# RMSNorm with gamma and Silu on one core: 64 KB runs in three buffers, gamma alone on VectorE, Silu by row with a scale, no look-ahead

## Chip, cores, metric

One core of a Trainium2 chip. The metric is the device time of one execution in microseconds (us).

## The reference, cut

```python
# x: 8 x 1024 x 2048 float32, gamma: 2048 float32, eps = 1e-5
rms = np.sqrt(np.mean(x ** 2, axis=-1, keepdims=True) + eps)
out = gamma * x / rms
return out * (1 / (1 + np.exp(-out)))          # Silu
```

There are 8192 rows of 8 KB. Every row is read once and written once: 67.1 MB in, 67.1 MB out. Nothing is reused except gamma.

## The kernel before

A block is 512 rows: four consecutive rows (32 KB) in each of 128 partitions, 4.2 MB. There are 16 blocks and six buffers. Loads are issued from ScalarE, stores from SyncE. The squares of a block are shared between ScalarE (`Square` with an accumulator) and VectorE; ScalarE takes the root, VectorE inverts it, VectorE multiplies by the reciprocal and gamma in one instruction per row, ScalarE applies Silu to two rows at a time.

```python
    J = 4
    BUFS = 6
    xb = x2.rearrange("(b p j) d -> b p (j d)", p=P, j=J)
    ...
    def load(b):
        xt = pool.tile([P, J * d], f32, name="xt")
        nc.scalar.dma_start(out=xt, in_=xb[b])
    ...
    def multiply(b):
        for j in range(J):
            nc.vector.scalar_tensor_tensor(out=row(b, j), in0=row(b, j), scalar=rstds[b][:, j:j + 1],
                                           in1=g, op0=ALU.mult, op1=ALU.mult)

    def silu(b):
        for h in range(0, J, 2):
            cols = slice(h * d, (h + 2) * d)
            nc.scalar.activation(out=blocks[b][:, cols], in_=blocks[b][:, cols], func=ACT.Silu)
        store(b)
    ...
        for b in range(last):                       # look-ahead: squares of b+1 before or beside block b
            loads = [b + 3] if BUFS <= b + 3 < nblk else []
            ...
            elif b < last - 1:
                squares_scalar(b + 1, loads)
                squares_vector(b + 1)
                root(b + 1)
                multiply(b)
                silu(b)
```

## Time and profile before

| | kernel before |
|---|---|
| time, median of 3 | 316.8 us (316.8 to 316.83) |
| span of the profile | 315.1 us |
| VectorE / ScalarE busy | 235.3 us (75%) / 213.8 us (68%) |
| DMA queues, share of 16 engines | 49.7% + 49.3% |

How to read it. A row of the 40 slices gives the busy share of an engine in each fortieth of the span, in tenths, 9 meaning 90% or more. The line of a DMA queue gives packets, MB, and the share of the 16 engines' time that its packets took. If the two queues together fill the span and the engines' rows have holes, the transfers set the time. The lines themselves stand in the prediction.

### The profile page before, as it was taken

How to read it: one execution, taken by the hardware profiler on the slowest of the kernel's cores; microseconds unless marked ns; L12 is line 12 of the kernel's file. 1: busy time of each engine (PE TensorE's matmuls, PEld its weight loads, DVE VectorE, ACT ScalarE, POOL GpSimd, SP SyncE). 2: the span in 40 equal slices, each digit the busy share in tenths (PEclk: the TensorE clock that was granted, in tenths of full speed). 3: DMA queues.
4: the chain of work that ended last, by engine and by line, in shares of the span. 5: the costliest groups of instructions: out<-in, count | busy, mean ns of one | idle time of the engine just before them, and what ended most of it. 6: DMA issues, size and time to landing. Idle time of an engine off the chain costs nothing.

```text
span 315.1 us, 436 instructions
## 1 busy us (share of the span) xinstructions
PE 2.1 (1%) x8; PEld 0.5 (0%) x8; DVE 235.3 (75%) x157; ACT 213.8 (68%) x136; POOL 0.2 (0%) x4
## 2 busy tenths in 40 slices
PE   0200000000000000000000000000000000000000
PEld 0000000000000000000000000000000000000000
DVE  0679597979995695957969489693995939999600
ACT  1349998972799258682687827877288768779910
POOL 0000000000000000000000000000000000000000
DMA  8999999999999999999999999999999999999996
GB/s 334 403 462 403 395 466 399 466 403 462 403 463 403 459 412 453 412 453 420 445 420 445 424 441 424 441 424 441 428 437 437 428 445 420 445 420 445 420 449 287
DMA packets 4618, 134.24 MB, mean 426 GB/s; under 512 B 516, under 2 KB 516, under 8 KB 520
## 3 DMA queue, kind: packets, MB, share of 16 engines
q10 hardware_dynamic: 2304, 67.11, 49.7%
q1 hardware_dynamic: 2312, 67.12, 49.3%
q14 instruction: 2, 0.02, 0.0%
HBM read 67.12 MB, written 67.11 MB: 426 GB/s over the span
## 4 chain that ended last, share of the span: by engine, by line
DMA 68%; DVE 14%; ACT 11%; issue 2%; ACTq 1%; DVEq 0%
DMA xt<-in_x_dram 68%; DVE xt L93 9%; DVE junk_v L74 5%; ACT xt L99 4%; ACT junk_a L66 3%; ACT xt L157 2%; ACT L83 1%; ACTq L190 1%; ACT L157 0%; ACT L99 0%; ACT rms L83 0%; DVE ss L74 0%; DVE rstd L88 0%; ACTq L55 0%; ACTq L83 0%
## 5 line engine op out<-in xcount | busy, mean ns | idle before, releaser
L93 DVE SCALAR_TENSOR_TENSOR xt<-xt,rstd,g 128x2048 f32<-128x2048 f32 x60 | 137.0, 2347 | 0.1
L99 ACT ACTIVATE xt<-xt 128x4096 f32<-128x4096 f32 x30 | 108.3, 3615 | 27.2 <-DVE xt L93 27.1
L74 DVE CUSTOM_DVE_ANT_0 junk_v<-xt 128x2048 f32<-128x2048 f32 x37 | 85.1, 2299 | 42.5 <-DMA xt<-in_x_dram 41.7
L66 ACT ACTIVATE junk_a<-xt 128x2048 f32<-128x2048 f32 x27 | 50.7, 1877 | 22.6 <-DMA xt<-in_x_dram 22.3
L83 ACT ACT_TABLE_LOAD x15 | 19.2, 1283 | 27.6 <-DVE ss L74 27.5
L99 ACT ACT_TABLE_LOAD x14 | 18.0, 1283 | 0.2
L118 DVE COPY g<-junk_v 128x2048 f32<-128x2048 f32 x1 | 2.3, 2292 | 9.4 <-PE junk_v L116 9.4
L88 DVE RECIPROCAL rstd<-rms 128x4 f32<-128x4 f32 x16 | 2.8, 174 | 8.3 <-ACT rms L83 8.3
L155 DVE TENSOR_TENSOR xt<-xt,g 128x2048 f32<-128x2048 f32 x4 | 8.9, 2279 | 0.0
L83 ACT ACTIVATE rms<-ss,eps_t 128x4 f32<-128x4 f32 x16 | 4.8, 297 | 5.7 <-DVE ss L74 5.5
L157 ACT ACTIVATE xt<-xt,rstd 128x2048 f32<-128x2048 f32 x4 | 7.7, 1990 | 0.0
L74 DVE DVE_READ_ACCUMULATOR2_ANT ss<- 128x1 f32 x37 | 5.2, 141 | 0.0
L66 ACT ACTIVATION_READ_ACCUMULATOR junk_a<-xt 128x1 f32 x27 | 5.0, 186 | 0.0
L111 ACT ACT_TABLE_LOAD x1 | 1.3, 1283 | 3.8 <-issue 3.8
L116 PE MATMUL junk_v<-grow,ones 1*128 1x512 f32 x8 | 2.1, 1130 | 8.2 <-DMA grow<-in_gamma_dram 8.2
L157 ACT ACT_TABLE_LOAD x1 | 1.3, 1283 | 0.0
L109 DVE MEMSET ones<- 128x128 f32 x1 | 0.2, 165 | 0.8 <-PEq L176 0.8
L116 PEld LDWEIGHTS junk_v<-grow,ones 1*128 1x128 f32 x8 | 0.5, 307 | 8.2 <-issue 8.2
L111 ACT ACTIVATE junk_a<-ones 128x1 f32<-128x1 f32 x1 | 0.2, 174 | 0.0
L176 POOL MEMSET const-bfloat16-1.0<- 128x1 bf16 x1 | 0.1, 101 | 0.0
L176 POOL MEMSET const-uint8-127<- 128x1 uint8 x1 | 0.1, 101 | 0.0
L176 POOL MEMSET const-float32-0.0<- 128x1 f32 x1 | 0.1, 98 | 0.2 <-issue 0.2
(2 smaller groups left out, 0.2 us busy)
## 6 DMA issues: line engine op xcount, KB each, us to landing
xt<-in_x_dram ACTq DMA_DIRECT2D x16, 4096.0 KB, 38.7
out_dram<-xt SPq DMA_DIRECT2D x16, 4096.0 KB, 29.0
grow<-in_gamma_dram SPq DMA_DIRECT2D x1, 8.0 KB
```

The source lines that it names most:

```text
L66: nc.scalar.activation(out=junk_a, in_=row(b, j), func=ACT.Square, accum_out=sss[b][:, j:j + 1])
L74: nc.vector.tensor_tensor_reduce(out=junk_v, in0=row(b, j), in1=row(b, j), scale=1.0, scalar=0.0, op0=ALU.mult, op1=ALU.add, accum_out=sss ...
L83: nc.scalar.activation(out=rms, in_=sss.pop(b), func=ACT.Sqrt, scale=1.0 / d, bias=eps_t)
L88: nc.vector.reciprocal(out=rstd, in_=rmss.pop(b))
L93: nc.vector.scalar_tensor_tensor(out=row(b, j), in0=row(b, j), scalar=rstds[b][:, j:j + 1], in1=g, op0=ALU.mult, op1=ALU.mult)
L99: nc.scalar.activation(out=blocks[b][:, cols], in_=blocks[b][:, cols], func=ACT.Silu)
L111: nc.scalar.activation(out=junk_a[:, 0:1], in_=ones[:, 0:1], func=ACT.Square)
L116: nc.tensor.matmul(junk_v[:, c * w:(c + 1) * w], ones[k:k + 1, :], grow[k:k + 1, :], start=True, stop=True)
L118: nc.vector.tensor_copy(out=g, in_=junk_v)
L155: nc.vector.tensor_mul(out=row(last, j), in0=row(last, j), in1=g)
L157: nc.scalar.activation(out=row(last, j), in_=row(last, j), func=ACT.Silu, scale=rstds[last][:, j:j + 1])
L190: with _tile.TileContext(nc) as tc:
```

## The change

It asks for longer runs in HBM (64 KB: eight rows per partition), fewer and larger transfers, fewer switches of ScalarE's tables, and a simpler order: load, squares, root, multiply, Silu, store, tile after tile, with no work on the next tile ahead of time. VectorE multiplies by gamma alone, two rows per instruction, and need not wait for the root; the reciprocal enters as the scale of Silu. The first and the last tile are cut in halves (and the last store in 4, 2, 2 rows).

```diff
-    J = 4
-    BUFS = 6
+    R = 8
+    BUFS = 3
+    xs = x2.rearrange("(s p r) d -> s p (r d)", p=P, r=R)
 ... (os likewise, for the output)
+    loads_of = [[R] for _ in range(nsup)]
+    stores_of = [[R] for _ in range(nsup)]
+    loads_of[0] = stores_of[0] = [4, 4]
+    loads_of[nsup - 1] = [4, 4]
+    stores_of[nsup - 1] = [4, 2, 2]
 ... (in load)
+        for lo, hi in pieces(loads_of[s]):
+            nc.scalar.dma_start(out=xt[:, cols(lo, hi)], in_=xs[s][:, cols(lo, hi)])
 ... (in group(s, lo, hi): squares of the first half of the rows on ScalarE, of the second on VectorE, root)
+        for r in range(lo, hi, 2):
+            if r == lo + 2:
+                nc.vector.reciprocal(out=rstd[:, 0:k], in_=rms[:, 0:k])
+            two = xt[:, cols(r, r + 2)].rearrange("p (r d) -> p r d", r=2)
+            nc.vector.tensor_mul(out=two, in0=two, in1=g.unsqueeze(1).to_broadcast([P, 2, d]))
+        for r in range(lo, hi):
+            row = xt[:, cols(r, r + 1)]
+            nc.scalar.activation(out=row, in_=row, func=ACT.Silu, scale=rstd[:, r - lo:r - lo + 1])
+            for a, b in pieces(stores_of[s]):
+                if b == r + 1:
+                    nc.sync.dma_start(out=os[s][:, cols(a, b)], in_=xt[:, cols(a, b)])
 ... (the loop)
+        for s in range(nsup):
+            for lo, hi in pieces(loads_of[s]):
+                group(s, lo, hi)
+            if s >= 1 and s + 2 < nsup:
+                load(s + 2)
```

More of the change, by code (lines that the diff above doesn't have):

```diff
@@ L31 @@
     n, d = x2.shape
-    J = 4
-    BUFS = 6
-    nblk = n // (P * J)
-    xb = x2.rearrange("(b p j) d -> b p (j d)", p=P, j=J)
-    ob = o2.rearrange("(b p j) d -> b p (j d)", p=P, j=J)
+    R = 8
+    BUFS = 3
+    nsup = n // (P * R)
+    xs = x2.rearrange("(s p r) d -> s p (r d)", p=P, r=R)
+    os = o2.rearrange("(s p r) d -> s p (r d)", p=P, r=R)
+    loads_of = [[R] for _ in range(nsup)]
[3 more added lines that the diff above has]
+    stores_of[nsup - 1] = [4, 2, 2]
     singles = ctx.enter_context(tc.tile_pool(name="singles", bufs=1))
@@ L44 @@
     w = d // Q
-    grow = singles.tile([P, w], f32)
     g = singles.tile([P, d], f32)
@@ L50 @@
     junk_v = psum.tile([P, d], f32, name="junk_v")
-    blocks, sss, rmss, rstds = {}, {}, {}, {}
-    def load(b):
-        xt = pool.tile([P, J * d], f32, name="xt")
-        nc.scalar.dma_start(out=xt, in_=xb[b])
-        blocks[b] = xt
-    def row(b, j):
-        return blocks[b][:, j * d:(j + 1) * d]
-    def squares_scalar(b, loads=()):
-        sss[b] = small.tile([P, J], f32, name="ss")
-        for j in range(share(b)):
-            nc.scalar.activation(out=junk_a, in_=row(b, j), func=ACT.Square,
-                                 accum_out=sss[b][:, j:j + 1])
-            if j == 0:
-                for s in loads:
-                    load(s)
@@ L72, in squares_vector @@
-    def squares_vector(b):
-        for j in range(share(b), J):
-            nc.vector.tensor_tensor_reduce(
-                out=junk_v, in0=row(b, j), in1=row(b, j), scale=1.0, scalar=0.0,
-                op0=ALU.mult, op1=ALU.add, accum_out=sss[b][:, j:j + 1])
-    def share(b):
-        return 1 if 4 <= b <= 12 and b % 2 == 0 else 2
-    def root(b):
-        rms = small.tile([P, J], f32, name="rms")
-        nc.scalar.activation(out=rms, in_=sss.pop(b), func=ACT.Sqrt, scale=1.0 / d, bias=eps_t)
-        rmss[b] = rms
@@ L86, in invert @@
-    def invert(b):
-        rstd = small.tile([P, J], f32, name="rstd")
-        nc.vector.reciprocal(out=rstd, in_=rmss.pop(b))
-        rstds[b] = rstd
-    def multiply(b):
-        for j in range(J):
-            nc.vector.scalar_tensor_tensor(out=row(b, j), in0=row(b, j), scalar=rstds[b][:, j:j + 1],
-                                           in1=g, op0=ALU.mult, op1=ALU.mult)
-    def silu(b):
-        for h in range(0, J, 2):
-            cols = slice(h * d, (h + 2) * d)
-            nc.scalar.activation(out=blocks[b][:, cols], in_=blocks[b][:, cols], func=ACT.Silu)
-        store(b)
@@ L102, in store, with cols, pieces, load @@
-    def store(b):
-        nc.sync.dma_start(out=ob[b], in_=blocks[b])
+    tiles = {}
+    def cols(lo, hi):
+        return slice(lo * d, hi * d)
+    def pieces(sizes):
+        lo = 0
+        for k in sizes:
+            yield lo, lo + k
+            lo += k
+    def load(s):
+        xt = pool.tile([P, R * d], f32, name="xt")
+        for lo, hi in pieces(loads_of[s]):
+            nc.scalar.dma_start(out=xt[:, cols(lo, hi)], in_=xs[s][:, cols(lo, hi)])
+        tiles[s] = xt
+    def group(s, lo, hi):
+        xt = tiles[s]
+        k = hi - lo
+        mid = lo + k // 2
+        ss = small.tile([P, R], f32, name="ss")
+        rms = small.tile([P, R], f32, name="rms")
+        rstd = small.tile([P, R], f32, name="rstd")
+        for r in range(lo, mid):
+            nc.scalar.activation(out=junk_a, in_=xt[:, cols(r, r + 1)], func=ACT.Square,
+                                 accum_out=ss[:, r - lo:r - lo + 1])
+        for r in range(mid, hi):
+            nc.vector.tensor_tensor_reduce(
+                out=junk_v, in0=xt[:, cols(r, r + 1)], in1=xt[:, cols(r, r + 1)], scale=1.0, scalar=0.0,
+                op0=ALU.mult, op1=ALU.add, accum_out=ss[:, r - lo:r - lo + 1])
+        nc.scalar.activation(out=rms[:, 0:k], in_=ss[:, 0:k], func=ACT.Sqrt, scale=1.0 / d, bias=eps_t)
+        for r in range(lo, hi, 2):
[9 more added lines that the diff above has]
+                    nc.sync.dma_start(out=os[s][:, cols(a, b)], in_=xt[:, cols(a, b)])
@@ L105 @@
     with tc.manual_schedule():
-        for b in range(BUFS):
-            load(b)
+        for s in range(BUFS):
+            load(s)
         nc.vector.memset(ones, 1.0)
@@ L111 @@
         nc.scalar.activation(out=junk_a[:, 0:1], in_=ones[:, 0:1], func=ACT.Square)
-        nc.sync.dma_start(out=grow[0:P:P // Q, :],
-                          in_=bass.AP(tensor=gamma.tensor, offset=gamma.offset, ap=[[w, Q], [1, w]]))
+        nc.sync.dma_start(out=g[0:1, :], in_=bass.AP(tensor=gamma.tensor, offset=gamma.offset, ap=[[d, 1], [1, d]]))
         for c in range(Q):
-            k = c * (P // Q)
-            nc.tensor.matmul(junk_v[:, c * w:(c + 1) * w], ones[k:k + 1, :], grow[k:k + 1, :],
+            nc.tensor.matmul(junk_v[:, c * w:(c + 1) * w], ones[0:1, :], g[0:1, c * w:(c + 1) * w],
                              start=True, stop=True)
         nc.vector.tensor_copy(out=g, in_=junk_v)
-        last = nblk - 1
-        SOON = 3
-        squares_scalar(0)
-        squares_vector(0)
-        root(0)
-        invert(0)
-        for b in range(last):
-            loads = [b + 3] if BUFS <= b + 3 < nblk else []
-            if b < SOON:
-                multiply(b)
-                squares_scalar(b + 1, loads)
-                silu(b)
-                squares_vector(b + 1)
-                root(b + 1)
-            elif b < last - 1:
-                squares_scalar(b + 1, loads)
-                squares_vector(b + 1)
-                root(b + 1)
-                multiply(b)
-                silu(b)
-            else:
-                multiply(b)
-                squares_scalar(b + 1)
-                silu(b)
-                squares_vector(b + 1)
-                root(b + 1)
-            if b + 1 < last:
-                invert(b + 1)
-        for j in range(J):
-            if j == J // 2:
-                invert(last)
-            nc.vector.tensor_mul(out=row(last, j), in0=row(last, j), in1=g)
-        for j in range(J):
-            nc.scalar.activation(out=row(last, j), in_=row(last, j), func=ACT.Silu,
-                                 scale=rstds[last][:, j:j + 1])
-        store(last)
+        for s in range(nsup):
[3 more added lines that the diff above has]
+                load(s + 2)
 _INS = ['x', 'gamma', 'eps']
```

## The prediction

> **What bounds the kernel now.** I read the page's header and its engine shares first, then the 40 slices, then the DMA queues, then the chain that ended last, and only then the groups. The page of the kernel before:
>
> ```profile
> span 315.1 us, 436 instructions
> ...
> PE 2.1 (1%) x8; PEld 0.5 (0%) x8; DVE 235.3 (75%) x157; ACT 213.8 (68%) x136; POOL 0.2 (0%) x4
> ...
> DVE  0679597979995695957969489693995939999600
> ACT  1349998972799258682687827877288768779910
> ...
> DMA  8999999999999999999999999999999999999996
> ...
> q10 hardware_dynamic: 2304, 67.11, 49.7%
> q1 hardware_dynamic: 2312, 67.12, 49.3%
> ...
> DMA 68%; DVE 14%; ACT 11%; issue 2%; ACTq 1%; DVEq 0%
> ```
>
> VectorE and ScalarE have slack (75% and 68%), and their slices are full of holes. The DMA row is at 9 in every slice but the first and the last, and the two queues together hold 99.0% of the 16 engines' time. So the DMA engines are never without work, from the first load to the last store. The chain says "DMA 68%", which understates it: where the chain walks through VectorE or ScalarE, the DMA row shows the engines busy all the same.
>
> Now the floor. In the trace's packet records the 4096 data packets are 32 KB each (four rows of one partition), and after the first ones nearly every one took 1.213 us, loads and stores alike. 4096 / 16 engines x 1.213 = 310.5 us. The 516 four-byte completion writes at 9 ns add 516 / 16 x 0.009 = 0.3 us. That leaves 315.1 - 310.8 = **4.3 us** that is not packets: about 2.0 us until the first packet moves, 0.7 us because the first ones are slow (about 1.9 us), 1.0 us from the last packet to the end of the span, and 0.6 us of small gaps. No change to the work on the engines can win more than a part of those 4.3 us (1.4%) unless it changes the packets. The measured time, 316.8 us, is 1.7 us over the span of the profile; I add that at the end.
>
> The rows of the groups that I price the change with:
>
> ```profile
> L93 DVE SCALAR_TENSOR_TENSOR xt<-xt,rstd,g 128x2048 f32<-128x2048 f32 x60 | 137.0, 2347 | 0.1
> L99 ACT ACTIVATE xt<-xt 128x4096 f32<-128x4096 f32 x30 | 108.3, 3615 | 27.2 <-DVE xt L93 27.1
> L74 DVE CUSTOM_DVE_ANT_0 junk_v<-xt 128x2048 f32<-128x2048 f32 x37 | 85.1, 2299 | 42.5 <-DMA xt<-in_x_dram 41.7
> L66 ACT ACTIVATE junk_a<-xt 128x2048 f32<-128x2048 f32 x27 | 50.7, 1877 | 22.6 <-DMA xt<-in_x_dram 22.3
> ...
> L155 DVE TENSOR_TENSOR xt<-xt,g 128x2048 f32<-128x2048 f32 x4 | 8.9, 2279 | 0.0
> ...
> L157 ACT ACTIVATE xt<-xt,rstd 128x2048 f32<-128x2048 f32 x4 | 7.7, 1990 | 0.0
> ```
>
> The last block of the kernel before already runs the scheme of the change (gamma alone on VectorE, Silu by row with a scale), so both new instruction forms have a measured duration here. The long idle times stand against the loads, as they should under a DMA bound.
>
> **What the Trainium skill says.** "DMA: Bandwidth & Descriptors", section Where 436 GB/s comes from, puts the ceiling of the 16 ports at 435.2 GB/s. The trace agrees: 32768 B / 1.213 us x 16 = 432 GB/s. At the ceiling 134.2 MB would take 308.4 us, so longer packets could win 2 us at most (an estimate from that page's figure). The same page, section Queues, rings and completion order, says that each engine goes round robin between its rings packet by packet; the packet records agree, load and store packets mostly alternate while both queues hold work. "ScalarE: Activation LUTs", section What ACT_TABLE_LOAD costs, gives 1283 ns for a table load; the trace shows 1283. "VectorE: DVE Perf Modes", section The perf-mode tier table, keeps an fp32 product of two tensors at the 1x rate, 2293 ns for 2048 elements; here it took 2279. So multiplying by gamma alone is barely cheaper than the fused form (2347).
>
> **The change part by part.**
>
> 1. Traffic: the same bytes. I take a 64 KB run to be one packet (my choice; two packets of 32 KB would change little). If the 1.213 us holds a fixed part of 8 ns over the ceiling rate (32768 B at 27.2 GB/s is 1.205 us), halving most packets saves about 100 x 8 ns per engine, **0.8 us**. The sum of packet time stays near 310.
> 2. VectorE: 37 squares become 32, (37 - 32) x (2.299 + 0.141) = -12 us; 64 multiplies of a row become 32 of two rows, some 32 x 4.46 = 143 against 146 us. Busy goes from 235 to about 221 us, all beside the transfers: worth nothing by itself.
> 3. ScalarE: squares 27 to 32, +10 us; Silu from 30 x 3.615 + 4 x 1.99 = 116 to 64 x 1.99 = 127, +11; table loads 31 to 21 (counted in the order of the built instructions: one switch each to the square root and to Silu for ten groups, and the first), -13. Busy about 222 us. Also beside the transfers.
> 4. Look-ahead gone: each group is now a serial chain. For eight rows, from data to last Silu: four VectorE squares 2.40 apart, 9.6; multiplies of pairs 4 x 4.46 with the reciprocal 0.18 between, to 27.6; two last Silu at 1.92 (7.68 / 4), **31.5 us**. For four rows: 4.8 + 0.18 + 8.92 + 3.84 = **17.7 us**. Storing waits for the whole tile.
> 5. Three buffers of eight rows hold as much as six of four. Load s+2 stands on ScalarE behind group s and waits for the store of tile s-1. In the steady part a load and a store of 8.4 MB share the engines for 2 x 16 x 1.213 = 38.8 us, and the chain needs 31.5: 7 us of slack a tile, so a store is queued before the previous one is out.
> 6. Start: the first four rows land at 12.8 us as now, the first store goes at 12.8 + 17.7 = 30.5 (35.2 before), the second at 47.5. Loads 0 to 2 are queued at once, as before. With loads and stores sharing packet by packet, tile 1 lands near 45, tile 2 near 74, the store of tile 0 ends near 80, and the store of tile 1 is issued at 45 + 31.5 = 76.5, just before the queues would run dry.
> 7. End: by the same bookkeeping tile 6 lands near 240, and from there the work is serial: 31.5 + 17.7 + 17.7 less about 1.5 of overlap = 65.4, to 305.4; then 1.2 us until the last two rows per partition move and 4.9 us to move them (8 packets of 0.61): 311.5 to 312.5. The transfers left at 240 take about 73 us, to 313. So the two end nearly together.
>
> I kept these books packet by packet, varying the depth of packets already committed to a ring, the issue latency (1 to 2 us) and the compute durations by a few per cent: the engines stood idle for 0 to 4 us in all, mostly at one tile boundary and before the last stores. Sum for the span: 310 of packets + 4.3 of ends and gaps + 1.5 of idle = 315.8; plus 1.7 gives **317.5 us**, a ratio of 1.002.
>
> **Rivals.** *A wait takes the place of the look-ahead.* ScalarE now stands at the load's wait for a store, and a whole 8.4 MB tile lands before any of its rows is touched. For it: the margins in 6 and 7 are 1 to 4 us, and one slip feeds the tail, where nothing hides it. Against: 7 us of slack per tile lets it recover. If two or three boundaries open, 3 to 8 us: 320 to 325. *Longer packets run nearer the ceiling*: at most 2 us won, 315. For it: only 64 KB runs; against: 432 of 435 GB/s already. *The HBM likes the 64 KB pitch less*: the start address steps double. No trace here tests that pitch; 1% slower packets would be 320. *Compute becomes the bound*: 222 us of busy on either engine in 315 speaks against it everywhere but in the last 70 us.
>
> **Range and chances.** The low end, 315, is no idle and faster packets; a gain over 2% would need 6.3 us of the 4.3 + 2.4 that are not packets at the ceiling, which is nearly excluded. The high end, 321.5, is one extra exposed boundary of about 4 us. Slower by over 2% (323.1) needs two of the rivals together. I give 0.01, 0.93 and 0.06.
>
> **What would show each step.** Right: the DMA row at 9 from slice 2 to 39, the queues' shares summing to about 98 to 99%, fewer packets (about 2300 data packets if a run is one packet), first store near 31 us, VectorE near 221 and ScalarE near 222 us busy. Wrong: a slice of the DMA row at 7 or less around 75 to 80, 157 or 270 us; packets longer per byte than 1.213 us per 32 KB; or a chain whose last 70 us is VectorE and ScalarE with DMA holes beside it. What would make the prediction wrong is mainly step 7, a later landing of tile 6.

## The result

The changed kernel took 321.68 us (median of 6 runs, 319.87 to 322.1) against 316.82 us. The ratio is 1.014, 95% interval 1.0119 to 1.0161. A ratio in this document is the mean time of one kernel's fast runs over the mean of the other's fast runs of the same rounds, so not quite the ratio of the medians quoted. A second set of five runs (e1 below) gave 1.0171. The kernel is slower by about 1.5%, within the 2% of "same" but clear of noise; I had put the centre at 1.002.

The page of the changed kernel, in the same views as before (span; busy time; the slices; the queues; the chain):

```profile
span 318.1 us, 389 instructions
...
PE 7.2 (2%) x8; PEld 2.5 (1%) x8; DVE 217.2 (68%) x109; ACT 218.3 (69%) x160; POOL 0.2 (0%) x4
...
DVE  0698739997989201999279960699706999687800
ACT  1379789688699601878776981678826688979730
...
DMA  8999799999999999999999999999999999999995
...
q10 hardware_dynamic: 1440, 67.11, 49.7%
q1 hardware_dynamic: 1586, 67.12, 48.8%
...
DMA 55%; DVE 28%; ACT 9%; issue 3%; ACTq 1%; DVEq 0%
```

VectorE and ScalarE still have slack (68% and 69%), and the DMA row is at 9 in every slice but the first, the fifth and the last (before: all but the first and the last). The two queues still hold 98.5% of the engines' time. Yet the span is 3.0 us longer for the same bytes. So the transfers did not wait much; they took longer. The 7 of slice 5 is mostly bookkeeping of long packets (slices 4 and 5 are listed at 527 and 284 GB/s, their mean is 406), but something happens there, as the packets show.

The groups that were priced came out as priced:

```profile
L89 DVE TENSOR_TENSOR xt<-xt,g 128x4096 f32<-128x4096 f32 x32 | 140.0, 4407 | 7.8 <-ACT junk_a L78 7.8
L92 ACT ACTIVATE xt<-xt,rstd 128x2048 f32<-128x2048 f32 x64 | 124.4, 1994 | 22.2 <-DVE rstd L87 13.7
```

The packet records of the two traces show where the 3 us are. (A packet here is one record: one run of one partition. After each transfer the records have 16 writes of four bytes, one per engine; I call them completion writes. Packet times are counted from a start up to 0.3 us earlier than that of the profile's views; only differences between them are read.) The records carry no engine number; I chained each packet to the one that ended where it began, to within 4 ns. Here is one engine at the moment when its first store packet comes (L load, S store, KB; start in us, duration):

```
before:  L32 37.01 1.21 | L32 38.22 1.81 | S32 40.03 1.21 | L32 41.24 1.21 | S32 42.45 1.21
after:   L64 29.45 2.42 | L64 31.87 3.20 | S32 35.07 1.21 | L64 36.28 3.21 | S32 39.49 1.21 | L64 40.70 2.42
```

At this place packets are stretched: one, by 0.6 us, before; two, by 0.8 us each, after. In the kernel before this happens once, and until the loads end neither queue is empty again. In the changed kernel it happens again when an empty queue gets work: near 86 us (load 3 was issued at 82.15 us, while the load queue had been dry since 77) and near 160 us. The sums, as means over the 16 engines, all from the packet records:

| us | before | after | after, second profile (e1) |
|---|---|---|---|
| time of all packets | 311.9 | 313.2 | 314.1 |
| of it, over the usual duration of their size | 1.3 | 3.3 | 4.2 |
| last completion write, median engine | 313.5 | 314.8 | 315.3 |
| last completion write, last engine | 314.2 | 317.0 | 319.0 |
| span | 315.1 | 318.1 | 320.0 |

Two terms grow: stretched packets (+2.0 and +2.9 us, less 0.7 that longer packets save) and the lag of the last engine behind the median one (0.7 before, 2.2 and 3.7 after). The lag can be seen in the windows view, whose last two columns are the DMA share and the GB/s. The last 9 us of the second profile of the changed kernel, then the last 8 of the kernel before:

```profile
310.00:314.00 4.00, 0.00 (x0) 0.00 (x0) 0.00 (x0) 0.00 (x0) 0.00 (x0) 1.00 1.05 451
314.00:319.00 5.00, 0.00 (x0) 0.00 (x0) 0.00 (x0) 0.00 (x0) 0.00 (x0) 1.00 0.24 102
```

```profile
307.00:311.00 4.00, 0.00 (x0) 0.00 (x0) 0.00 (x0) 0.00 (x0) 0.00 (x0) 1.00 1.10 475
311.00:315.00 4.00, 0.00 (x0) 0.00 (x0) 0.00 (x0) 0.00 (x0) 0.00 (x0) 1.00 0.36 156
```

(A share over 1 is again a packet counted whole.) In the changed kernel most engines are done from 315.3 us on; by the records the last two of the sixteen work on, to 319.0. No compute was left to wait for: the last Silu ended at 305.2 us in the first profile, and store packets followed each other until the end.

### The profile page after: what moved, and what is told of

Read it like the earlier page. It is cut to its first block, busy times and chain, and to the rows that moved or that the text cites.

```text
span 318.1 us, 389 instructions
## 1 busy us (share of the span) xinstructions
PE 7.2 (2%) x8; PEld 2.5 (1%) x8; DVE 217.2 (68%) x109; ACT 218.3 (69%) x160; POOL 0.2 (0%) x4
## 4 chain that ended last, share of the span: by engine, by line
DMA 55%; DVE 28%; ACT 9%; issue 3%; ACTq 1%; DVEq 0%
DMA xt<-in_x_dram 31%; DMA out_dram<-xt 24%; DVE xt L89 22%; ACT xt L92 7%; DVE junk_v L81 6%; ACT junk_a L78 2%; ACTq L144 1%; DVE ss L81 0%; DVE rstd L87 0%; DVEq L144 0%; DVEq L81 0%; ACTq L66 0%
## 5 line engine op out<-in xcount | busy, mean ns | idle before, releaser
L89 DVE TENSOR_TENSOR xt<-xt,g 128x4096 f32<-128x4096 f32 x32 | 140.0, 4407 | 7.8 <-ACT junk_a L78 7.8
L92 ACT ACTIVATE xt<-xt,rstd 128x2048 f32<-128x2048 f32 x64 | 124.4, 1994 | 22.2 <-DVE rstd L87 13.7
L81 DVE CUSTOM_DVE_ANT_0 junk_v<-xt 128x2048 f32<-128x2048 f32 x32 | 73.6, 2299 | 65.2 <-DMA xt<-in_x_dram 64.5
L78 ACT ACTIVATE junk_a<-xt 128x2048 f32<-128x2048 f32 x32 | 60.1, 1879 | 52.9 <-DMA xt<-in_x_dram 48.8
L105 PE MATMUL junk_v<-g,ones 1*128 1x512 f32 x8 | 7.2, 1073 | 2.8 <-DMA g<-in_gamma_dram 2.8
L78 ACT ACTIVATION_READ_ACCUMULATOR junk_a<-xt 128x1 f32 x32 | 6.0, 186 | 0.0
L81 DVE DVE_READ_ACCUMULATOR2_ANT ss<- 128x1 f32 x32 | 4.5, 140 | 0.0
L84 ACT ACTIVATE rms<-ss,eps_t 128x8 f32<-128x8 f32 (+1 forms) x10 | 3.0, 299 | 0.1
L87 DVE RECIPROCAL rstd<-rms 128x8 f32<-128x8 f32 (+1 forms) x10 | 1.9, 186 | 1.2 <-ACT rms L84 1.2
L105 PEld LDWEIGHTS junk_v<-g,ones 1*128 1x128 f32 x8 | 2.5, 326 | 5.9 <-issue 5.9
```

The lines of the kernel that those rows point to most:

```text
L78: nc.scalar.activation(out=junk_a, in_=xt[:, cols(r, r + 1)], func=ACT.Square, accum_out=ss[:, r - lo:r - lo + 1])
L81: nc.vector.tensor_tensor_reduce(out=junk_v, in0=xt[:, cols(r, r + 1)], in1=xt[:, cols(r, r + 1)], scale=1.0, scalar=0.0, op0=ALU.mult, op ...
L84: nc.scalar.activation(out=rms[:, 0:k], in_=ss[:, 0:k], func=ACT.Sqrt, scale=1.0 / d, bias=eps_t)
L87: nc.vector.reciprocal(out=rstd[:, 0:k], in_=rms[:, 0:k])
L89: nc.vector.tensor_mul(out=two, in0=two, in1=g.unsqueeze(1).to_broadcast([P, 2, d]))
L92: nc.scalar.activation(out=row, in_=row, func=ACT.Silu, scale=rstd[:, r - lo:r - lo + 1])
```

## The experiments

Four theories stood after the two traces. **P**: 64 KB packets themselves (stretched packets, engines that drift apart). **H**: the HBM serves the 64 KB pitch more slowly (the pitch is the distance in HBM from the run of one partition to that of the next). **L**: without look-ahead the queues run dry. **T**: the serial compute of the last 70 us sets the end. T had no support in the trace, since there was no hole before the last stores, and no run was spent on it alone.

### e1: the changed kernel again

No edit.

> The changed kernel unaltered, for a second profile and a tighter ratio. Theory P (64 KB packets: the 16 engines, which alternate load and store packet by packet, drift apart, transfers are complete only when the last engine is, and the pauses at a change from one queue to two are longer): ratio 1.010 to 1.017; the completion writes of one transfer again spread over 1.3 to 4 us (at most 1.0 in the kernel before), and the last engine ends some 2 us after the median one. Theory T (the serial compute of the last 70 us ends last): a hole in the DMA row before the last two stores, which the first profile did not show.

Measured: 322.38 us, ratio 1.0171 (1.0158 to 1.0184). The 16 completion writes of one transfer spread over up to 4.5 us in the steady part and over 11 us for the last load; in the kernel before, never over more than 1.0. The last engine was 3.7 us behind the median one. This agrees with P, and so do the table's sums above. Even where it misses (11 us), it is in the direction of P.

### e2: each 64 KB transfer as two of 32 KB

```diff
-            nc.scalar.dma_start(out=xt[:, cols(lo, hi)], in_=xs[s][:, cols(lo, hi)])
+            for c in range(lo, hi, 4):
+                nc.scalar.dma_start(out=xt[:, cols(c, c + 4)], in_=xs[s][:, cols(c, c + 4)])
 ... (the stores likewise, both halves issued where the one store stood)
```

> The changed kernel with every transfer of eight rows issued as two of four rows at the same place: packets of 32 KB, the 64 KB pitch in HBM, the buffers, the order and the moment of every store kept. Theory P (packet size): most of the 4.4 us comes back, ratio 1.000 to 1.007, and the spread of the completion writes falls to 1.5 us or less. Theory H (the 64 KB pitch makes HBM slower) and theory L (loss of the look-ahead: stores come in bursts, so queues run dry or change more often): ratio stays at 1.010 to 1.017.

Measured: 318.92 us (317.33 to 320.28), ratio 1.0058 (1.0036 to 1.0081). About two thirds of the loss came back, which agrees with P. Stretched packets fell to 1.5 us and the last engine was 0.9 us behind the median. The spread of the loads' completion writes fell only to 2.15 us, more than the 1.5 expected.

The run has a flaw: "the moment of every store kept" is not so. A store of half a tile waits for its own four rows alone. In the timeline of e12, which has such stores, the first half of tile 3 leaves at 164.7 us and the last row is done at 173.3, so it has a start of 8.6 us. This holds for every run with 32 KB stores of eight-row tiles (e2, e4, e5, e8, e12), not for those with 64 KB stores (e1, e6, e7). So only runs with the same stores can be compared strictly, and what e2 won may be due to the packets or to the earlier half.

### e3: the kernel before with the 64 KB pitch

```diff
-    xb = x2.rearrange("(b p j) d -> b p (j d)", p=P, j=J)
+    xs = x2.rearrange("(s p r) d -> s p (r d)", p=P, r=2 * J)
+    xb = [xs[b // 2][:, (b % 2) * J * d:(b % 2 + 1) * J * d] for b in range(nblk)]
 ... (ob likewise)
```

> The kernel before with its 4-row blocks taken as halves of 8-row runs: 32 KB packets as before, but the pitch from partition to partition is 64 KB. Theory P and theory L: unchanged, ratio 0.997 to 1.003. Theory H: 1.008 to 1.015, with 32 KB packets slower than 1.213 us.

Measured: 317.26 us, ratio 1.0011 (0.9999 to 1.0023); packets at 1.213 us as before. Theory H falls: the pitch costs 0.2% at most.

### e4: two halves, and the 32 KB pitch

```diff
-    xs = x2.rearrange("(s p r) d -> s p (r d)", p=P, r=R)
+    xb = x2.rearrange("(b p j) d -> b p (j d)", p=P, j=4)
 ... (as e2, with in_=xb[2 * s + c // 4]; stores likewise)
```

> As e2 (two transfers of 32 KB runs), and the pitch back at 32 KB as well, so that only three buffers of eight rows, the missing look-ahead and the new arithmetic are left of the change. Theory P: as e2, 1.000 to 1.007. Theory H: as the kernel before or 1.000 to 1.005 while e2 stays above 1.010. Theory L: 1.010 to 1.017 here too.

Measured: 317.97 us, ratio 1.0035 (1.0023 to 1.0047). So with 32 KB packets and the first half of a tile free to leave early, three buffers, no look-ahead and the new arithmetic together cost 0.35%. Theory L in its plain form (the order alone costs 1.0% or more) falls; that a whole tile leaves later than it could may still be part of the loss. The difference to e2 is within the overlap of the two intervals and is left open.

### e5: as e2, but nothing starts on half a tile

In e2, ScalarE could begin when the first half had landed. This run takes that away.

```diff
+        if k == R:
+            first, second = [4, 5, 0, 1], [6, 7, 2, 3]      # rows of the squares, ScalarE and VectorE
```

> e2 let ScalarE begin on a tile when its first half had landed. Here both engines begin with rows of the second half (ScalarE rows 4, 5, 0, 1, VectorE 6, 7, 2, 3), so nothing of a tile starts before all of it is there, as in the changed kernel; packets stay at 32 KB. If the packet size was the cause of the gain of e2: ratio 1.002 to 1.009, as e2. If the early start was: back at 1.012 to 1.018.

Measured: 318.92 us, ratio 1.0062 (1.0049 to 1.0074), the same as e2. That ScalarE began early was not the reason. (The earlier store of the first half remains here.)

### e6: only the loads of tiles 1 and 2 in halves

In the changed kernel the 32 KB stores of tile 0 meet 64 KB loads. If each queue gets one packet in turn, these stores have a third of the rate. (The rows of the squares are taken as in e5, here and in e7 and e8.)

```diff
+        step = 4 if s in (1, 2) else 8
+            for c in range(lo, hi, step):
```

> The changed kernel with only the loads of tiles 1 and 2 as two transfers of 32 KB runs (started on as in e5), all later loads and stores 64 KB. In the changed kernel the 32 KB stores of tile 0 alternate with 64 KB loads, so they get a third of the rate, tile 0 leaves at 82 us, load 3 waits for it and the load queue is dry from 77 to 86. If that unequal start is what costs: load 3 is issued near 74, the long packets near 85 are gone, ratio 1.000 to 1.009. If 64 KB packets cost throughout: 1.012 to 1.018.

Measured: 320.28 us, ratio 1.0112 (1.0087 to 1.0137), which no single expectation covered. The load queue was less dry after tile 2, yet stretched packets still came to 4.2 us in sum, most of them later, and the last engine was 2.2 us behind. If the two ratios, taken on different chips, may be subtracted, the uneven start is about a third of the loss (1.0171 to 1.0112) and the rest comes later.

### e7: stores 64 KB, loads 32 KB

```diff
+        step = 4                      # loads
 ...
+                    step = 8          # stores
```

> Only the stores keep 64 KB packets, loads are 32 KB (gated as e5). If unequal packets give the longer ones two thirds of the rate and leave the queues dry in turn: 1.008 to 1.02. If only the size of a packet at a change of queues counts: between e5 and the changed kernel, 1.006 to 1.012.

Measured: 327.71 us, ratio **1.0348** (1.0333 to 1.0363), twice the loss of the changed kernel. Now there is a real hole in the DMA row (windows view, DMA share in the last column but one):

```profile
150.00:159.00 9.00, 0.00 (x0) 0.00 (x0) 9.00 (x3) 8.17 (x5) 0.00 (x0) 1.00 1.01 437
159.00:164.00 5.00, 0.00 (x0) 0.00 (x0) 3.26 (x2) 4.56 (x4) 0.00 (x0) 1.00 0.48 164
```

VectorE waits 26 us for tile 3 (timeline, one line; idle time before it and what ended it in brackets):

```profile
135.08 2.30 DVE L87 CUSTOM_DVE_ANT_0 junk_v<-xt 128x2048 f32<-128x2048 f32 x1 [26.09 <-DMA xt<-in_x_dram]
```

Tile 3 lands late because the stores take the larger share. The packet records show the share: from 90 to 130 us 178 load and 176 store packets started, one in turn, and the loads moved 149 GB/s, the stores 283 (e5 in the same time: 266 and 262 packets, 217 and 215 GB/s). Before the arithmetic of tile 3 is done, the queued stores are out, tile 4 has all but landed, and little is left to transfer.

The order of the program has a part in the hole. Load 5 takes the buffer of tile 2, whose store was out at 147.6 us by the packet records, but it stands on ScalarE behind tile 3's work and was issued only 14 us later, when the store of tile 3 was still to come:

```profile
162.01 0.82 ACTq L69 DMA_DIRECT2D xt<-in_x_dram  x2
...
165.92 0.33 SPq L104 DMA_DIRECT2D out_dram<-xt  x1
```

In e1, e5 and e8 load 5 followed the end of that store within 0.6 us. What the share would cost if loads did not stand behind the arithmetic, no run shows.

### e8: loads 64 KB, stores 32 KB

```diff
+        step = 8                      # loads
 ...
+                    step = 4          # stores
```

> The mirror of e7: loads keep 64 KB packets, all stores are 32 KB. If the alternation by packets hands the longer packets two thirds of the rate, stores now lag, buffers come free late and the load queue runs dry at each tile: the chain of waits shows loads waiting for stores, ratio 1.015 to 1.04. If unequal sizes do no harm of their own: 1.006 to 1.013.

Measured: 317.86 us, ratio **1.0023** (1.0009 to 1.0036), the best of all variants of the change. This expectation was wrong in both branches. The stores did lag and loads did wait for stores, as the first branch said (the waits view has 31.5 us of ScalarE waiting for a store); but the DMA row stays at 8 or 9 up to the last slice, since the engines have stores to move meanwhile. From 88 to 102 us the loads moved 300 GB/s and the stores 133. Tile 3 was there 19.5 us earlier than in e7:

```profile
115.63 2.30 DVE L87 CUSTOM_DVE_ANT_0 junk_v<-xt 128x2048 f32<-128x2048 f32 x1 [7.26 <-DMA xt<-in_x_dram]
```

With e12, told below, and the rest:

| ratio to the kernel before | stores 32 KB, first half early | stores 64 KB, whole tile |
|---|---|---|
| loads 16 KB | 1.0457 (e12) | |
| loads 32 KB | 1.0062 (e5) | 1.0348 (e7) |
| loads 64 KB | 1.0023 (e8) | 1.0171 (e1) |

Down each column the stores are the same and only the load packets grow; the time falls each time, by 1.7% in the right column and by 3.8 and 0.4% in the left. Theory P, by which 64 KB packets are bad as such, says the opposite, and the pitch is the same in all five. From left to right two things change, packet size and the early half, so that direction is not proof. (e5, e7 and e8 take the rows of the squares in one order, e1 and e12 in their own; e2 and e5, which differ in that order alone, gave 1.0058 and 1.0062.)

### e9 and e10: a copy with 64 KB packets, and with 32 KB

Wrong results: the arithmetic is left out, each tile of eight rows is loaded and stored as it is, with three buffers. e10 stores the second half first and loads the first half first, so that its waits are for whole tiles as in e9.

```diff
-        (squares, root, multiply, Silu, stores by row)
+        nc.sync.dma_start(out=os[s], in_=xt)        # e9; e10: as two of four rows, (4, 0)
```

> Wrong result on purpose: no arithmetic, each tile of eight rows is loaded and stored as it is, 64 KB packets, three buffers. If 64 KB packets on two queues cost by themselves (engines drift apart, the last one is late): ratio 1.006 or more and a spread of the last completion writes of 2 us or more. If they cost only through the chain between landing and store: 0.995 to 1.003, and the packet time alone would even save 0.7 us.

> Wrong result on purpose: the copy of e9 with each transfer as two of 32 KB runs, issued in an order that keeps the waits of the whole tile (second half stored first, first half loaded first). If 64 KB packets cost by themselves: 0.997 to 1.004 here against 1.0112 of e9, and the spread of the completion writes of a half at most 2 us. If the copies suffer from three buffers and late issue whatever the packet: 1.008 to 1.014 again.

Measured: e9 320.67 us, ratio 1.0112 (1.0098 to 1.0126); e10 316.71 us, ratio 0.9993 (0.9981 to 1.0006). They ran on different chips, each against the kernel before beside it. So 64 KB packets in both queues cost about 1.2% with no arithmetic at all. How, as far as the records tell: between packets the engines of e9 stood idle for 1.8 us on the mean, those of e10 for next to nothing, and stretched packets came to 2.7 us against 1.3. In e10 the writes of each transfer spread over 0.5 us at most; in e9 the spread grows to 6 us. A store may begin only when the last engine has its part of the tile. The last tile's load had ended on the median engine at 291.8 us and on the last at 295.2; meanwhile the store queue had run out (294.5 on the median engine). e9 and e10 in the same stretch, windows view:

```profile
293.00:297.00 4.00, 0.00 (x0) 0.00 (x0) 0.00 (x0) 0.00 (x0) 0.00 (x0) 1.00 0.65 279
```

```profile
293.00:297.00 4.00, 0.00 (x0) 0.00 (x0) 0.00 (x0) 0.00 (x0) 0.00 (x0) 1.00 0.91 393
```

The lag of the last engine at the end, which I had expected to be 2 us or more, was 1.1 us in e9: there the drift of the engines had turned into this hole.

### e11: the kernel before with 16 KB packets

```diff
+        for c in range(0, J * d, 2 * d):
+            nc.scalar.dma_start(out=xt[:, c:c + 2 * d], in_=xb[b][:, c:c + 2 * d])
 ... (stores likewise)
```

> The kernel before with every transfer of four rows issued as two of two rows: 16 KB packets. They took 0.611 us in the tails of the runs so far, so 512 x 0.611 = 312.8 us against 256 x 1.213 = 310.5: 2.3 us more, less about 0.3 for the shorter stretched packet at the first store. Expected ratio 1.004 to 1.009. If shorter packets were better throughout, below 1.000.

Measured: 319.12 us, ratio 1.0068 (1.0055 to 1.0081), as worked out from 0.611 us a packet. Shorter is not better: of the even sizes tried, 32 KB is the best.

### e12: loads 16 KB, stores 32 KB

e7 at half the size, to separate share from size. Each load of tiles 1 to 6 is two transfers with a gap in them, so that a packet is two rows.

```diff
+            to = xt.rearrange("p (h q c) -> p h q c", h=2, q=2)
+            at = xs[s].rearrange("p (h q c) -> p h q c", h=2, q=2)
+            for q in range(2):
+                nc.scalar.dma_start(out=to[:, :, q, :], in_=at[:, :, q, :])
 ... (stores 32 KB; squares of rows 6, 7, 0, 1 on ScalarE, 2 to 5 on VectorE)
```

> So far: loads/stores in KB 64/64 1.017, 32/32 1.006, 64/32 1.002, 32/64 1.035. This one has 16 KB load packets for tiles 1 to 6 (each transfer takes rows 0, 1, 4, 5 or 2, 3, 6, 7 of a partition) and 32 KB stores: e7 at half the size, everything gated on both transfers. If what counts is that longer store packets take two thirds of the rate and starve the loads (theory S, share): 1.02 to 1.04, tile 3 landing after 130 us, as e7. If it is the absolute size of 64 KB packets (theory P): 1.005 to 1.012, of which up to 0.003 for the fixed cost of short packets.

Measured: 331.66 us, ratio **1.0457** (1.0439 to 1.0476), the slowest of all, with no packet over 32 KB. Tile 3 came at 142.5 us, and the hole followed (timeline, then windows):

```profile
142.51 2.30 DVE L94 CUSTOM_DVE_ANT_0 junk_v<-xt 128x2048 f32<-128x2048 f32 x1 [29.75 <-DMA xt<-in_x_dram]
...
164.69 9.00 SPq L111 DMA_DIRECT2D out_dram<-xt  x2
```

```profile
159.00:168.00 9.00, 0.00 (x0) 0.00 (x0) 9.00 (x3) 8.16 (x5) 0.00 (x0) 1.00 0.41 175
```

This is the share again: from 90 to 135 us the loads moved 170 GB/s and the stores 254, the queue with the longer packets getting the larger part. If that is the store queue, tiles land late and the serial chain from landing to the first store (142.5 to 164.7 us, the two lines of the timeline) is exposed: VectorE and ScalarE are busy in the row of the windows view, the DMA engines stand at 0.41. As in e7, load 5 came late as well (its buffer was free at 143.5 us, it was issued at 169.50). e5 has the same stores and 32 KB loads, and no such hole (its windows view over the same stretch):

```profile
159.00:168.00 9.00, 0.00 (x0) 0.00 (x0) 1.36 (x1) 1.36 (x1) 0.00 (x0) 1.00 1.04 448
```

The hole is not the whole loss. Over their usual durations the packets took 6.9 us in e7 and 6.5 in e12, against 2.6 in e5 and 2.1 in e8. And engines drift without 64 KB packets too: the completion writes of one transfer spread over up to 5.8 us in e12 and 3.4 in e5.

## Why the prediction was right or wrong

**Right: the bound, the class, the compute.** The transfers bound both kernels, and the ratio stayed within 2%. VectorE came to 217.2 us busy (221 predicted), ScalarE to 218.3 (222). The books of landings held within about 3 us: first store at 30.2 us (31), tile 1 at 48.3 (45), tile 2 at 77.3 (74), store of tile 1 at 79.1 in the second profile (76.5), tile 6 at 240.9 (240), last Silu at 305.2 (305.4). The saving of 8 ns over two shorter packets was there: a 64 KB packet took 2.418 us, 2 x 1.213 is 2.426. The rival of the pitch fell with e3, the rival of compute as a bound with the trace. One count was off: "about 2300 data packets" were 2688 (1536 of 64 KB, 896 of 32 KB, 256 of 16 KB).

**Wrong: step 1 and the term of 1.5 us of idle.** The step that failed reads: "I take a 64 KB run to be one packet (my choice; two packets of 32 KB would change little)". One packet it was; but with two of 32 KB the time went from 322.38 to 318.92 us (e1, e2, same rounds; with the flaw told at e2), and in the copies, which have no such flaw, from 320.67 to 316.71 us. And the sum had "310 of packets + 4.3 of ends and gaps + 1.5 of idle". Between first and last packet there was no idle time in the packet records of the changed kernel. In its place stood stretched packets (packets that took longer than the usual duration of their size), 3.3 and 4.2 us where the kernel before had 1.3, and the last engine's lag, 2.2 and 3.7 us where it had 0.7. I had treated the 16 engines as one in the books, so neither could appear. Yet the first was in the trace of the kernel before: of the 4.3 us outside the packets I had booked 0.6 as "small gaps", but its engines were idle for only about 0.1 us between packets, and the packets stretched at the first store, near 38 us, are 0.65 us. The median came out just above the upper end of the range (321.68 to 321.5; 322.38 in e1), so that the class held is in part luck: the reason was not among the rivals. The nearest, "a wait takes the place of the look-ahead", foresaw idle engines at tile boundaries; the boundaries did show, near 86 and 160 us, but as stretched packets.

**What is shown, and what is only seen.** Shown by runs: 64 KB in both queues costs 1.2% without any arithmetic (e9, e10), so with arithmetic packet size can be a good part of the 1.7%; with the stores kept the same, and but for the order of the squares, longer load packets help and shorter ones hurt, at 64 and at 32 KB stores (e1 and e7; e8, e5 and e12), and the queue with the longer packets has the higher rate; the pitch costs 0.2% at most (e3). Seen in the traces but not isolated by a run: that packets stretch when a queue that was empty on an engine gets work, and that a few engines end late. Open: how the 1.7% of e1 divides between the packet size, the unequal start (0.6%, by e6) and the store that waits for a whole tile; why those engines are late and not others; what makes engines drift, since 64 KB loads beside 32 KB stores (e8) did no harm and e12 drifted without them; how much of e7 and e12 is the load's place behind the arithmetic; and the 0.2 to 0.35% that e8 and e4 keep over the kernel before. No variant beat the kernel before: e3 and e10 equal it within their intervals, and e10 computes nothing.

## What to carry to other kernels

When loads and stores share the DMA engines and both queues are full, look at the packet size of each queue: here it set the share of the rate (149 to 283 GB/s in e7). In this kernel load packets at least as long as store packets were the better side, since a late load exposed the compute behind it while a late store was hidden by the next load; and a load that stands behind arithmetic in its engine's program makes the hole longer. A longer run was worth only the fixed part of a packet (8 ns in 2426), while completion waits for the slowest of 16 engines, and in the copies these drifted apart by 6 us at 64 KB, by 0.5 at 32. A DMA share of 98% is not proof that the floor is reached: sum the packet durations and look at the last engine, too.

## What the Trainium skill lacked or had wrong

- "DMA: Bandwidth & Descriptors", section Queues, rings and completion order, says that an engine takes turns between rows by whole packets of some 9 to 17 descriptors. In the records here the turn is one record, a run of one partition of 16, 32 or 64 KB (178 load and 176 store packets from 90 to 130 us of e7); how many descriptors a record holds they do not say. The page does not draw the consequence that unequal runs divide the rate unequally (149 to 283 GB/s in e7): with 32 KB stores, the ratio was 1.0457 at 16 KB loads, 1.0062 at 32 and 1.0023 at 64.
- The same page, Rules for kernel authors, asks for transfers of at least 1 MiB; no upper limit on the run is named. Here 64 KB runs in both queues made a plain copy 1.2% slower than 32 KB runs (e9, e10), and 16 KB runs made the kernel before 0.7% slower (e11).
- No page has the stretched packet: a packet in flight when the other queue joins took 1.8 instead of 1.21 us (32 KB) and 3.2 instead of 2.42 us (64 KB).
- No page gives a number for how far the 16 engines of one transfer drift apart. Here it was 1.0 us at most in the kernel before, up to 11 us in the changed one.
